# Moving the value products of a group of keys behind the next group's transposes

## The chip, the cores and the metric

The kernel runs on one core of a Trainium2 chip. The metric is the device time of one execution in microseconds (us). Before the change it is 2855.03 us, the median of three runs (2853.68 to 2860.54). The profile comes from one execution of its own.

The engines are PE (TensorE: matrix products and transposes, with PEld for the loading of weights), DVE (VectorE), ACT (ScalarE), POOL (GpSimd) and SP (SyncE, which issues the DMAs here). Each works through its own queue in order. PE writes to PSUM; ACT and DVE read it from there.

## The reference

Two layers (DEPTH) over 2048 frames of width 1024. Each layer normalises x, projects it once, and gives the columns to two groups of four heads; both outputs are concatenated, sent through one output projection, and added to x. A last RMSNorm closes the trunk.

```python
h = rmsnorm(x, norm_w)
proj = einsum('bsd,de->bse', h, w_in)
mq, mk, mv, mi, mf, mz, aq, ak, av, az = split(proj)
# mLSTM heads: causal conv + SiLU on q and k, chunkwise matrix memory, RMSNorm, skip, gate
ym = (rmsnorm(mlstm_chunkwise(conv(mq), conv(mk), mv, mi, mf)) + m_skip * conv(mq)) * silu(mz)
# differential attention: two maps per head, block-causal mask in chunks of 64
p = softmax(where(mask, q k^T / 8, -inf))          # for both maps
a = p[map 0] - lam * p[map 1]
ya = rmsnorm(a @ v) * (1 - lambda_init) * silu(az)
x = x + concat(ym, ya) @ w_out
```

What the change touches is the product `a @ v`, which the text calls the value products. It computes the same numbers before and after.

## The kernel before, in words

**Tiles and units.** The sequence is cut into 4 tiles of 512 frames. A unit is one layer, one tile and one head pair (one mLSTM head and one attention head of the same number): 2 x 4 x 4 = 32 units. All products use operands split in a high and a low part (`hth`/`htl` of the input, `wh`/`wl` of the weights, `ath`/`atl` of the map), three products for one.

**Attention of a unit.** `scores` (L654) computes, for two query blocks of 128 (a pair) and both maps, the scores against all key tiles so far; DVE copies them out of PSUM with their maximum (L706, tile `p`), ACT takes the exponential (L669), and DVE combines the two maps into one (L683). `apply_v` (L722) then handles the combined map in groups of 256 keys. For a group, `ta` (L741) lets PE transpose four blocks of 128 x 128 (L109, tile `tpa`, three blocks at the diagonal, with a memset of the fourth at L748), ACT copies the result out as the high part `ath` (L755), and DVE subtracts it from PSUM to give the low part `atl` (L756). `tb` (L760) then issues the six value products of the group (tile `pv`). There are 288 groups in 64 pairs.

**Buffers.** `tpa` has one buffer in PSUM, `pv` one, `sc` (scores) two, `mm` (projections) three, `ml` one. `ath` and `atl` have two each in SBUF. So the transposes of the next group can begin only when ACT and DVE have both read `tpa`, and a group's copy-out can begin only when the value products two groups before are done.

**The order of the work.** A planner gives every task a due time in its own units, and the tasks are recorded in the order of these times (L1083). Four streams are kept: P (projections and output projections, which fill PE), A (scores), V (transposes, value products, `finish`), and M (the mLSTM). `pin` (L90) ties PE's instructions of a stream into a chain in recorded order; P is also tied behind whatever the other streams had due 15 units earlier. Between the streams a scheduler may order PE's instructions otherwise. On the other engines the copy-outs at L755 and L756 are recorded with a priority of 150 places (`HA`).

The due times of a pair's groups come from `put_v` (L947), with a spacing d of 3 to 6 units:

```python
for i, (ta, tb) in enumerate(gs):
    at(a + i * d, ta, "V")
    at(a + (i + VL) * d, tb, "V")
...
return a + (len(gs) - 1 + VL) * d
```

`VL` is the constant at L40. What `put_v` returns sets the due time of `finish` (L771), of the next pair's first group, and, through `ve + 2.0` and `fin_t`, the earliest due time of the second half of the next value projection and of an output projection.

**The end.** After the last unit, P holds the rest of the output projection of the last tile; its last part (L828 to L845) needs `yha` and `yla` of the last head, which come from the last value products by `ot` (L766), transposes of `ot`, and L792. Then `final_last` (L866) normalises the rows.

Of the kernel before, what the change touches and what calls it, by code (L numbers as in the profile page):

```python
# [36 lines left out]
QL = 0.8  # L37
VF = 0.8
VD = 3.0
VL = 0.6  # L40
FD = 5.5
XD = 10.0
MD = 9.0
# [9 lines left out]
def trunk_kernel(ctx, tc, x, w_ch, w_v0, w_v, w_o, nw, cw, cb, gb, mnw, msk, anw, lam,  # L53
# [893 lines left out]
    def put_v(gs, a, d, groups):  # L947
# [4 lines that stand above are left out]
            if i + 1 == len(gs) or groups[i + 1][0] != groups[i][0]:  # L952
                for _ in range(2):
                    heapq.heappush(p_free, a + i * d + 1.5)
        return a + (len(gs) - 1 + VL) * d

# [212 lines left out]
```

## Time and profile before

| | |
|---|---|
| median of the runs | 2855.03 us |
| the profiled execution | 2855.48 us |
| its span, first to last instruction | 2853.7 us |
| mean granted clock of TensorE | 0.980 of full speed |
| PE busy | 2675.9 us, 94% |
| DVE busy | 1873.5 us, 66% |
| ACT busy | 1641.3 us, 58% |
| POOL busy | 1422.6 us, 50% |

"Idle before" in a row is the time that the engine stood still before that instruction, and the arrow names what ended it. A wait for several things is put down to the last of them. The granted clock is 1.0 at 2.4 GHz and 0.5 at 1.2 GHz.

### The profile page before, as it was taken

The numbers are of one execution on the slowest core, as the hardware profiler recorded it, in microseconds if no ns is written. First come the engines' busy times: TensorE is split into PE (matmuls) and PEld (weight loads), VectorE is DVE, ScalarE is ACT, GpSimd is POOL, SyncE is SP. The second block draws the span as 40 slices with busy tenths as digits, with TensorE's granted clock in tenths as the row PEclk, the third lists the DMA queues.
The fourth block names the chain that finished last, engine by engine and source line by source line (L and its number), as shares of the span: only waits on it lengthen the run. The fifth ranks groups of instructions, "written<-read, shape, count | busy, mean of one in ns | idle before, by whom it ended". The sixth has DMA issues, their size and how long they took to land. (4 is left out here: it accounts for less than half of the span.)

```text
span 2853.7 us, 49241 instructions
## 1 busy us (share of the span) xinstructions
PE 2675.9 (94%) x16692; PEld 2376.0 (83%) x16692; DVE 1873.5 (66%) x4879; ACT 1641.3 (58%) x4407; POOL 1422.6 (50%) x1182
## 2 busy tenths in 40 slices
PE   7999899989999899989999999999999999998997
PEld 6898788878888888977889888888888888887877
DVE  5656565666757757676765466666577676776684
ACT  5555465655655556655655555555465555665664
POOL 5565656535554254434446656555554545445324
PEclk9999999999999999999999999999999999999998
DMA  6645655554653444433546455665447444465232
GB/s 202 173 137 159 187 156 146 152 186 137 181 142 121 152 130 131 140 93 116 163 143 182 141 171 151 198 185 148 144 144 233 139 140 146 115 200 159 82 99 87
DMA packets 248923, 428.91 MB, mean 150 GB/s; under 512 B 30304, under 2 KB 107104, under 8 KB 248672
## 3 DMA queue, kind: packets, MB, share of 16 engines
q1 hardware_dynamic: 248672, 425.77, 50.1%
q8 instruction: 132, 2.16, 0.3%
q14 instruction: 119, 0.97, 0.1%
HBM read 312.28 MB, written 63.05 MB: 132 GB/s over the span
## 5 line engine op out<-in xcount | busy, mean ns | idle before, releaser
L188 POOL TENSOR_TENSOR wl<-wr,wh 128x512 fp32r<-128x512 f32 (+1 forms) x676 | 898.9, 1335 | 1131.2 <-PE mm L106 523.3
L186 ACT ACTIVATE wh<-wr 128x512 fp32r<-128x512 f32 (+1 forms) x676 | 423.0, 628 | 411.0 <-PE mm L106 223.3
L106 PE MATMUL mm<-hth,wh 128*128 128x512 f32 x1536 | 621.7, 405 | 1.6 <-ACT vaug L337 1.4
L106 PE MATMUL mm<-htl,wh 128*128 128x512 f32 x1536 | 610.4, 397 | 0.0
L706 DVE TENSOR_SCALAR_CACHE_REDUCE p<-sc 128x512 f32<-128x512 f32 (+3 forms) x640 | 380.4, 605 | 130.3 <-PE sc L106 115.8
L669 ACT ACTIVATE p<-p,nm 128x512 f32<-128x512 f32 (+3 forms) x640 | 413.7, 649 | 80.8 <-DVE nm L665 79.7
L106 PE MATMUL mm<-hth,wl 128*128 128x512 f32 x1536 | 442.5, 401 | 0.0
L106 PEld LDWEIGHTS mm<-hth,wh 128*128 128x128 f32 x1536 | 292.1, 190 | 60.7 <-ACT vaug L337 2.3
L106 PEld LDWEIGHTS mm<-htl,wh 128*128 128x128 f32 x1536 | 291.7, 190 | 56.9
L106 PEld LDWEIGHTS mm<-hth,wl 128*128 128x128 f32 x1536 | 285.4, 190 | 60.9
L683 DVE SCALAR_TENSOR_TENSOR p<-p,s 128x512 f32<-128x512 f32 (+2 forms) x320 | 293.3, 962 | 2.3
L106 PE MATMUL mm<-wh,hth 128*128 128x256 f32 (+1 forms) x1024 | 268.0, 292 | 19.2 <-DVE gt L339 6.7
L755 ACT ACTIVATE ath<-tpa 128x512 fp32r<-128x512 f32 x288 | 170.4, 592 | 178.2 <-PE tpa L109 176.2
L106 PE MATMUL mm<-wh,htl 128*128 128x256 f32 (+1 forms) x1024 | 263.6, 288 | 0.0
L756 DVE TENSOR_TENSOR atl<-tpa,ath 128x512 fp32r<-128x512 f32 x288 | 197.0, 684 | 88.1 <-ACT ath L755 87.2
L106 PE MATMUL sc<-kp,q 128*128 128x512 f32 x768 | 245.9, 407 | 8.6 <-DVE p L706 8.4
L106 PEld LDWEIGHTS mm<-wh,hth 128*128 128x128 f32 x1024 | 198.8, 194 | 24.7 <-issue 10.7
L106 PEld LDWEIGHTS mm<-wh,htl 128*128 128x128 f32 x1024 | 198.8, 194 | 2.6
L109 PE MATMUL tpa<-ident,p 128*128 128x128 f32 x1088 | 186.6, 278 | 5.9 <-DVE tpa L748 4.5
L400 DVE SCALAR_TENSOR_TENSOR cacc<-mm,cw,cacc 128x511 f32<-128x511 f32 (+2 forms) x192 | 141.5, 737 | 72.2 <-ACT cacc L396 68.9
L106 PE MATMUL pv<-ath,vp 128*128 128x256 f32 x768 | 178.9, 287 | 1.4 <-ACT ath L755 1.4
L106 PE MATMUL mm<-wl,hth 128*128 128x256 f32 (+1 forms) x1024 | 168.6, 293 | 0.6 <-POOL wl L188 0.6
(202 smaller groups left out, 5672.6 us busy)
## 6 DMA issues: line engine op xcount, KB each, us to landing
wr<-in_w_ch_dram SPq DMA_DIRECT2D x384, 256.0 KB, 2.7
wr<-in_w_o_dram SPq DMA_DIRECT2D x132, 256.0 KB, 2.9
q<-ab SPq DMA_DIRECT2D x256, 128.0 KB, 2.4
vp<-vd SPq DMA_DIRECT2D x48, 512.0 KB, 4.5
wr<-in_w_v_dram SPq DMA_DIRECT2D x96, 256.0 KB, 3.4
kp<-kd SPq DMA_DIRECT2D x48, 512.0 KB, 3.7
wr<-in_w_v_dram SPq DMA_DIRECT2D x64, 264.0 KB, 3.1
kc<-ab SPq DMA_DIRECT2D x256, 64.0 KB, 2.0
```

What stands on the lines that cost most here:

```text
L106: pin(PE.matmul(o, l, r, start=start, stop=stop, skip_group_check=True))
L109: pin(PE.transpose(o, i, ident[:n, :n]))
L186: A.activation(wh[:, :n], wr[:, :n], AF.Copy)
L188: G.tensor_tensor(wl[:, :n], wr[:, :n], f32(wh[:, :n]), op=ALU.subtract)
L400: V.scalar_tensor_tensor(out=acc[:, d:], in0=ps[:, 0:T - d], scalar=w(j), in1=acc[:, d:], op0=ALU.mult, op1=ALU.add)
L669: A.activation(pp[:, :w], pp[:, :w], AF.Exp, bias=nm[:, m:m + 1], accum_out=zc[:, m, kt:kt + 1])
L683: V.scalar_tensor_tensor(out=pc[0][kt][:, :w], in0=pc[1][kt][:, :w], scalar=s_[:, 0:1], in1=pc[0][kt][:, :w], op0=ALU.mult, op1=ALU.add)
L706: V.tensor_scalar(out=pp[:, :w], in0=ps[:, :w], scalar1=0.125, scalar2=None, op0=ALU.mult, op1=ALU.max, accum_out=c["mx"][:, m, kt:kt + 1])
L755: A.activation(ah, p2, AF.Copy)
L756: V.tensor_tensor(al, p2, f32(ah), op=ALU.subtract)
```

## The change

One constant is changed; no instruction is added or removed.

```diff
 QL = 0.8
 VF = 0.8
 VD = 3.0
-VL = 0.6
+VL = 1.5
 FD = 5.5
```

A group's value products are due 1.5 spacings after its transposes instead of 0.6, so that the next group's transposes, due one spacing after, come ahead of them in the V chain. `put_v` returns a time that is later by 0.9 d.

PE, inside the attention of layer 1, tile 3, head 2, second pair, before: the transposes of a group (`tpa`), filling products of a projection (`mm`) and of scores (`sc`), then this group's own value products (`pv`), then the next group's transposes.

```order
L109 MATMUL tpa<-ident,p 128x128 x3
L106 MATMUL mm<-hth,wl 128x512 x2
L106 MATMUL mm<-hth,wh 128x512
L106 MATMUL mm<-htl,wh 128x512
L106 MATMUL sc<-kp,q 128x512 x4
L106 MATMUL pv<-ath,vp 128x256
L106 MATMUL pv<-atl,vp 128x256
L106 MATMUL pv<-ath,vp 128x256 x2
L106 MATMUL pv<-atl,vp 128x256
L106 MATMUL pv<-ath,vp 128x256
L109 MATMUL tpa<-ident,p 128x128 x4
```

The same place on PE in the changed kernel, the same names; the value products at the end are those of the first of the two groups.

```order
L109 MATMUL tpa<-ident,p 128x128 x4
L106 MATMUL mm<-hth,wh 128x512
L106 MATMUL mm<-htl,wh 128x512
L106 MATMUL mm<-hth,wh 128x512
L106 MATMUL mm<-htl,wh 128x512
L106 MATMUL mm<-hth,wl 128x512 x4
L106 MATMUL mm<-hth,wh 128x512
L106 MATMUL mm<-htl,wh 128x512
L106 MATMUL mm<-hth,wh 128x512
L106 MATMUL mm<-htl,wh 128x512
L109 MATMUL tpa<-ident,p 128x128 x4
L106 MATMUL pv<-ath,vp 128x256
```

The six value products went from just ahead of the next group's transposes to just behind them, and the first instruction that needs the copied-out group is now the next transposes.

PE at the end of the program, before: the last transposes of a map, four filling products, the last value products, the transposes of `ot`, and the first of the output projection's last part (`wh,yha`).

```order
L109 MATMUL tpa<-ident,p 128x128
L106 MATMUL mm<-wl,yha 128x256 x2
L106 MATMUL mm<-wl,yhm 128x256 x2
L106 MATMUL pv<-ath,vc 128x256
L106 MATMUL pv<-atl,vc 128x256
L106 MATMUL pv<-ath,vc 128x256 x2
L106 MATMUL pv<-atl,vc 128x256
L106 MATMUL pv<-ath,vc 128x256
L109 MATMUL tpa<-ident,ot 128x128 x4
L106 MATMUL mm<-wh,yha 128x256
```

The same end in the changed kernel, from the fillers ahead of the last value products on.

```order
L106 MATMUL mm<-wl,yha 128x256 x2
L106 MATMUL pv<-ath,vc 128x256
L106 MATMUL pv<-atl,vc 128x256
L106 MATMUL pv<-ath,vc 128x256 x2
L106 MATMUL pv<-atl,vc 128x256
L106 MATMUL pv<-ath,vc 128x256
L109 MATMUL tpa<-ident,ot 128x128 x2
L106 MATMUL mm<-wl,yhm 128x256 x2
L106 MATMUL mm<-wh,yhm 128x256
L106 MATMUL mm<-wh,ylm 128x256
L106 MATMUL mm<-wh,yhm 128x256
L106 MATMUL mm<-wh,ylm 128x256
```

Twenty filling products that stood ahead of the last value products now stand behind the first two transposes of `ot`, ahead of the other two.

## Rows read from the trace of the kernel before

**Rows 1.** The page, part 1 and two lines of part 2: busy time (share) and instructions of each engine, then PE's busy tenths and its granted clock in 40 slices of the span.

```profile
PE 2675.9 (94%) x16692; PEld 2376.0 (83%) x16692; DVE 1873.5 (66%) x4879; ACT 1641.3 (58%) x4407; POOL 1422.6 (50%) x1182
...
PE   7999899989999899989999999999999999998997
...
PEclk9999999999999999999999999999999999999998
```

**Rows 2.** The waits of PE over the whole span: who waited for whom, us in total, times, longest us.

```profile
PE pv L106 <- DVE atl L756: 52.8, 35, 5.6
PE mm L109 <- DVE x L239: 15.5, 4, 7.2
PE mm L106 <- DVE htl L273: 14.8, 7, 4.0
PE sc L106 <- DVE p L706: 11.7, 14, 2.5
...
PE pv L106 <- ACT ath L755: 6.4, 10, 2.0
...
PE tpa L109 <- DVE tpa L748: 4.5, 4, 1.6
```

**Rows 3.** PE in order of time in a quiet stretch: start, us, what (neighbours of one kind merged).

```profile
2500.02 0.39 PE L106 MATMUL mm<-htl,wh 128*128 128x512 f32 x1
2500.25 0.39 PE L106 MATMUL mm<-hth,wh 128*128 128x512 f32 x1
...
2501.65 0.28 PE L106 MATMUL pv<-ath,vp 128*128 128x256 f32 x1
2501.77 0.28 PE L106 MATMUL pv<-atl,vp 128*128 128x256 f32 x1
2501.88 0.39 PE L106 MATMUL pv<-ath,vp 128*128 128x256 f32 x2
2502.11 0.29 PE L106 MATMUL pv<-atl,vp 128*128 128x256 f32 x1
2502.24 0.28 PE L106 MATMUL pv<-ath,vp 128*128 128x256 f32 x1
2502.36 0.60 PE L109 MATMUL tpa<-ident,p 128*128 128x128 f32 x4
```

**Rows 4.** PE in order of time around one of the waits, with the idle time before an instruction and what ended it in brackets.

```profile
1294.04 0.28 PE L106 MATMUL pv<-ath,vp 128*128 128x256 f32 x1
1297.35 0.39 PE L106 MATMUL pv<-atl,vp 128*128 128x256 f32 x1 [3.03 <-DVE atl L756]
...
1299.68 0.63 PE L106 MATMUL mm<-hth,wh 128*128 128x512 f32 x1
1300.11 0.63 PE L106 MATMUL mm<-htl,wh 128*128 128x512 f32 x1
```

**Rows 5.** DVE in order of time in three stretches, the first before the wait of rows 4, the second before the longest kind of wait, the third before another wait of 3.0 us.

```profile
1292.70 3.99 DVE L683 SCALAR_TENSOR_TENSOR p<-p,s 128x512 f32<-128x512 f32 x3
1296.61 0.68 DVE L756 TENSOR_TENSOR atl<-tpa,ath 128x512 fp32r<-128x512 f32 x1
...
1214.02 6.75 DVE L683 SCALAR_TENSOR_TENSOR p<-p,s 128x512 f32<-128x512 f32 x4
1220.70 0.68 DVE L756 TENSOR_TENSOR atl<-tpa,ath 128x512 fp32r<-128x512 f32 x1
...
2691.66 4.66 DVE L683 SCALAR_TENSOR_TENSOR p<-p,s 128x512 f32<-128x512 f32 x4
2696.24 0.68 DVE L756 TENSOR_TENSOR atl<-tpa,ath 128x512 fp32r<-128x512 f32 x1
```

**Rows 6.** POOL in order of time beside the second and the third stretch of rows 5.

```profile
1213.92 1.29 POOL L436 TENSOR_TENSOR t<-t,ra 128x512 f32<-128x512 f32 x1
1215.18 1.72 POOL L188 TENSOR_TENSOR wl<-wr,wh 128x512 fp32r<-128x512 f32 x1
1216.85 3.37 POOL L442 TENSOR_TENSOR ab<-t,ab 128x512 fp32r<-128x512 f32 x2
...
2692.82 1.41 POOL L628 TENSOR_TENSOR ylm<-ytm,yhm 128x512 fp32r<-128x512 f32 x1 [1.22 <-ACT yhm L626]
2694.18 1.72 POOL L188 TENSOR_TENSOR wl<-wr,wh 128x512 fp32r<-128x512 f32 x1
```

**Rows 7.** Groups of instructions over the whole span: line, engine, what, count, then busy us, mean ns of one, idle time before and what ended it.

```profile
L683 DVE SCALAR_TENSOR_TENSOR p<-p,s 128x512 f32<-128x512 f32 (+2 forms) x320 | 293.3, 962 | 2.3
L755 ACT ACTIVATE ath<-tpa 128x512 fp32r<-128x512 f32 x288 | 170.4, 592 | 178.2 <-PE tpa L109 176.2
L756 DVE TENSOR_TENSOR atl<-tpa,ath 128x512 fp32r<-128x512 f32 x288 | 197.0, 684 | 88.1 <-ACT ath L755 87.2
```

**Rows 8.** Busy time in ten stretches at half clock, each right behind or around a wait of the value products: stretch and its length, busy us of PE, PEld, DVE, ACT, POOL (instructions), PE's granted clock, DMA share, GB/s; the last line has the sums.

```profile
629.10:639.30 10.20, 6.99 (x32) 6.69 (x32) 6.21 (x11) 3.70 (x9) 6.92 (x6) 0.50 0.51 160
...
1298.10:1301.50 3.40, 3.40 (x12) 2.82 (x11) 1.10 (x3) 0.60 (x1) 0.00 (x0) 0.50 0.07 25
...
2697.56:2700.97 3.41, 3.41 (x13) 2.93 (x12) 1.26 (x3) 0.60 (x1) 0.00 (x0) 0.50 0.09 35
sum 47.65, PE 40.48 PEld 35.16 DVE 28.53 ACT 16.09 POOL 18.66; mean PE 4.05 PEld 3.52 DVE 2.85 ACT 1.61 POOL 1.87
```

**Rows 9.** PE in order of time at the end of the program, from the last value products to the output projection's last part.

```profile
2826.35 0.39 PE L106 MATMUL pv<-ath,vc 128*128 128x256 f32 x1 [0.44 <-ACT ath L755]
2827.29 0.39 PE L106 MATMUL pv<-atl,vc 128*128 128x256 f32 x1 [0.55 <-DVE atl L756]
...
2828.62 0.44 PE L109 MATMUL tpa<-ident,ot 128*128 128x128 f32 x2 [0.25 <-ACT ot L766]
2830.43 0.39 PE L106 MATMUL mm<-wh,yha 128*128 128x256 f32 x1 [1.37 <-ACT yha L626]
2831.77 0.58 PE L106 MATMUL mm<-wh,yla 128*128 128x256 f32 x1 [0.96 <-POOL yla L628]
```

## The prediction

> **What bounds the kernel now.** I read the page first: PE is busy for 94% of the span, DVE, ACT and POOL for no more than 66%, and PE's granted clock falls below nine tenths in none of the 40 slices but the last [rows 1]. So time is won where PE waits, and where its clock is down. Next come PE's own waits. The largest entry is the value products waiting for DVE's subtraction of the low part of the transposed map: 52.8 us in 35 waits, the longest 5.6 us, and 6.4 us more in 10 waits for ACT's copy of the high part [rows 2]. That is 59.2 us; no other entry has more than 15.5 us. The timeline around one wait shows its form: the first value product needs only the high part and runs, the second needs the low part, and PE, which works in order, stands for 3.03 us [rows 4]. Then DVE before such waits: the subtraction itself takes 0.68 us, but it stood behind three or four combinations of the two maps, 3.99, 6.75 and 4.66 us of them [rows 5]. So the wait is a queue on DVE and not the subtraction's own length. Last the clock: behind or around these waits there are ten stretches, 47.65 us together, at half clock; in them PE was busy for 40.48 us [rows 8], and a 512-column product took 0.43 us from start to start [rows 4] where it otherwise takes 0.23 us [rows 3].
>
> **The window.** No instruction is added or removed, so PE's work is the same and only positions count. Before, a group's transposes are followed by filling products, then by this group's six value products, then by the next transposes. Afterwards the same fillers stand there, but the six value products in front of the next transposes are gone, and six of the group before have come in behind the first transposes. The wait does not go: `tpa` has one buffer, so the next transposes wait for the same subtraction in place of the value products. In 225 of the 288 groups they are, by the changed order, the first instruction that needs it; in the others, mostly the last group of a pair or one whose value products moved further, the value products still are. What is won is the length of the window. Six value products take 0.71 us from start to start (2501.65 to 2502.36) [rows 3], and this much work now stands between a group's transposes and the first need of its subtraction that did not stand there before. Counting both orders with the step lengths of rows 3 gives nearly that: the window is 4.3 us on average before and 4.9 us after.
>
> **Its worth in waits.** The 45 waits [rows 2] fall on 37 groups that waited for over 0.2 us and a few that waited less; 25 of the 37 waited longer than 0.71 us. These lose 0.71 us each (17.8 us), the other twelve lose all that they have (5.5 us): 23.3 of the 59.2 us. A second way, place by place: I kept each group's time from transposes to finished subtraction from the trace, and shifted its window by the difference of the two orders at this place. That saves 31.4 us and makes 8.1 us of new waits where the window has become shorter: net 23.3 us too. From one side the change could save nothing, since DVE's queue is refilled differently, and from the other all 59.2 us. I take -23.
>
> **Its worth in clock.** At half clock PE lost half of 40.48 us in those stretches, 20.2 us [rows 8]. 19 waits are over 1.2 us now, and 11 would be after 0.71 us is taken off. In proportion 8 of 19 of 20.2 us is 8.5 us. The long waits, which are the ones that stay, are the surest to be followed by such a stretch, so I take -6, between 0 and 20.
>
> **The end.** After the last value products PE has nothing to fill: it stands for 0.44, 0.55, 0.25, 1.37 and 0.96 us, 3.6 us in all [rows 9]. The changed order puts twenty 256-column products behind the first two transposes of `ot`; at 0.117 us each (the steps of rows 3) this is 2.3 us of work inside that chain. I take -2, between 0 and -3.6.
>
> **What is given back.** On DVE the scheduler's choice changes too. Before, three or more combinations stand among the five rows ahead of a subtraction at 22 places; after, at 33. Of the 22, six waited now, 21.6 us together (the two of 5.5 us and that of rows 4 among them), or 1.0 us for a place. Eleven more places would cost 11 us, and less the share that the longer window takes, 6.5 us; between 0 and 40 (all eleven at the mean 3.6 us of the six). I take +6. Scores have two buffers: the amount by which the PE work between a score tile and its buffer's next use falls short of 2 us adds up to 10.1 us over the order before and 16.6 us after. The wait that answers to it is 11.7 us [rows 2], so +7, between -5 and +15. ACT's side costs nothing: the copy-out takes 0.59 us, and ACT is idle for 178.2 us before it in waiting for the transposes [rows 7]. The buffers of `ath` and `atl` cost nothing either, since the transposes that lead to their reuse stand behind the value products that free them. The later due time of `finish` and of the next value projection shows only in the planner's units, as the projections that wait for it stand many units later; I count 0 for it, up to +5 at the change of layers, where the second half of a value projection is held back by 5 more units.
>
> A rule speaks against the window. The Trainium skill, in "PSUM — Partial Sum Buffer", section "Summary: rules for kernel authors", says that PSUM should be read while matrix products run into a different bank. With one buffer for `tpa` this change does the opposite and puts the next write to that bank in the queue ahead of useful products. By that rule alone the wait would be moved whole and nothing won; no row of before shows transposes waiting for this subtraction, so it stands as the first rival.
>
> A second page prices the queue on DVE higher. Four combinations took 6.75 us while POOL worked without a gap, 1.69 us each [rows 5, 6], against 0.96 us in the mean [rows 7]. The Trainium skill ("SBUF — State Buffer", section "SBUF: two separate sides") has a DVE instruction with two SBUF inputs and a POOL instruction that reads SBUF block each other for whole instructions. The trace agrees at this place. By it a place with four combinations ahead costs 6.8 us instead of 3.8 us, which makes the slower rival dearer by 3 us a place.
>
> **The sum.** -23 -6 -2 +6 +7 = -18 us. Against the profiled execution's own 2855.5 us this is 2837 us. Its time is 0.4 us over the median of the runs, which changes nothing.
>
> **The rivals.** *The wait moves whole* (chance 0.22). The transposes wait instead, DVE's queue being as long relative to PE as before because it is fed by PE's own progress. For it: the copies-out wait for PE for 176.2 us [rows 7], so the engines follow one another; against it: ACT and DVE do not have to wait for value products. Savings of 0 to 9 us, about what the extra places and the scores cost: 2847 to 2864, most likely 2854.
>
> *DVE's queue decides, and the kernel is slower* (0.21). The mechanism is the eleven added places where the subtraction stands behind three or four combinations, now with transposes and everything behind them held. If all cost 3.6 us, this is 40 us, with half clock after each (11 x 1.7 us, half of a 3.4 us stretch) 19 us more, against 31 us saved elsewhere: 2855.5 + 40 + 19 - 31 = 2883; with the half of them 2855.5 + 20 + 10 - 16 = 2869. It decides from about five of the eleven on.
>
> *The longer window clears most waits* (0.12). If the waits go to a quarter, as they might if the scheduler has put the copies-out well at the long waits, 44 us and 13 us of clock go with the 2 us of the end, less 7 us for scores: 2855.5 - 52 = 2803. Against it: the longest waits have four combinations in front and are eight times as long as what is gained.
>
> The forecast has 0.45, with 2815 to 2847 as its own range. A measurement of this kernel tells a difference of about 0.3%, 9 us, from none. Faster by more than that: the forecast's part below 2846.5 and the last rival, 0.56. Within it: 0.23. Slower: the second rival, 0.21. The range leaves out the lower half of the last rival and the upper half of the slower one: 2806 to 2868.
>
> **What would show it.** Right: the value products' wait for the subtraction falls to 15 us or less, a new entry of transposes waiting for the subtraction appears with 15 to 30 us, both together 32 to 42 us; the mean clock rises from 0.980 to about 0.984; scores wait for DVE for 15 to 20 us; PE stands for less than 2 us in the last chain. Wrong: the two waits together are still over 50 us (the wait moved whole) or over 70 us (DVE's queue), or other waits of PE, taken together, grow by more than 15 us.

## The result and the profile after

The changed kernel takes 2882.63 us (median of four runs, 2880.42 to 2891.37) against 2854.53 us before in the same session: on record a ratio of 1.0104, with a 95% interval of 1.0085 to 1.0123 (the two medians alone give 1.0098). It is 1.0% slower. The prediction said 2837 us, 2806 to 2868, and gave "slower" a chance of 0.21; it was wrong in sign, and the time lies outside the range. The ratios here and below leave out two runs that stood far off, one of a control (2979.87 us, at a clock of 0.937) and one of the kernel before (6880.96 us).

The profiled execution took 2883.08 us, its span is 2881.2 us, and the mean granted clock is 0.975 (before: 2855.48, 2853.7, 0.980). The page, part 1 and the two lines of part 2 that answer to [rows 1]:

```profile
PE 2686.6 (93%) x16692; PEld 2380.3 (83%) x16692; DVE 1883.6 (65%) x4879; ACT 1648.2 (57%) x4407; POOL 1426.9 (50%) x1182
...
PE   7999899989998899999999999999999999999987
...
PEclk9999999999999999999999999999999999999999
```

The counts are the same, so the work is. The span grew by 27.5 us: PE's busy time by 10.7 us (the same instructions, at a mean clock of 0.975 instead of 0.980), and its idle time, span less busy, from 177.8 to 194.6 us, 16.8 us more. The waits of PE, to be held against [rows 2] (who waited for whom, us in total, times, longest us):

```profile
PE sc L106 <- DVE p L706: 31.7, 23, 3.3
PE tpa L109 <- DVE atl L756: 30.0, 20, 4.5
...
PE pv L106 <- DVE atl L756: 14.0, 5, 4.3
PE ml L106 <- DVE C L587: 12.8, 7, 2.7
PE tpa L109 <- DVE tpa L748: 12.6, 11, 5.6
...
PE sc L106 <- DMA kc<-ab: 5.7, 2, 5.4
PE sc L106 <- DMA q<-ab: 4.9, 1, 4.9
...
PE pv L106 <- ACT ath L755: 2.3, 2, 1.3
...
PE mm L106 <- DVE htl L273: 1.1, 2, 0.7
```

The entry that the change was aimed at looks as forecast. The value products' 52.8 us became 14.0, the transposes have a new 30.0, and with the wait for `ath` the three fell from 59.2 to 46.3 us, 12.9 us less (a later run shows that this fall is not the swap's). But all other idle time grew by 16.8 + 12.9 = 29.7 us: scores waiting for DVE from 11.7 to 31.7, scores waiting for loads from nothing to 10.6, `ml` for `C` from 4.8 to 12.8, the memset of `tpa` from 4.5 to 12.6; `htl` fell from 14.8 to 1.1. Most of the loss lies in three stretches of layer 1, each between the same two ACT instructions (L423) in both kernels. Their busy times in the kernel before: stretch and length, busy us of PE, PEld, DVE, ACT, POOL (instructions), granted clock, DMA share, GB/s; the last line has the sums:

```profile
2114.90:2227.00 112.10, 108.43 (x698) 97.00 (x698) 86.17 (x217) 71.23 (x207) 53.92 (x44) 0.97 0.67 206
2293.90:2412.70 118.80, 110.57 (x721) 99.64 (x720) 83.64 (x219) 68.41 (x174) 55.49 (x45) 0.97 0.51 154
2483.50:2603.20 119.70, 112.61 (x747) 101.51 (x746) 88.86 (x224) 77.31 (x219) 53.64 (x44) 1.00 0.58 181
sum 350.60, PE 331.61 PEld 298.14 DVE 258.67 ACT 216.96 POOL 163.05; mean PE 110.54 PEld 99.38 DVE 86.22 ACT 72.32 POOL 54.35
```

The same three in the changed kernel:

```profile
2120.20:2242.10 121.90, 109.98 (x698) 98.19 (x697) 88.52 (x218) 70.81 (x205) 53.87 (x44) 0.94 0.60 190
2308.90:2433.70 124.80, 113.80 (x729) 102.45 (x729) 82.09 (x219) 70.15 (x175) 56.47 (x45) 0.95 0.49 147
2502.70:2628.60 125.90, 117.96 (x749) 104.76 (x748) 91.16 (x227) 80.39 (x226) 54.58 (x44) 0.96 0.56 169
sum 372.60, PE 341.74 PEld 305.40 DVE 261.76 ACT 221.35 POOL 164.92; mean PE 113.91 PEld 101.80 DVE 87.25 ACT 73.78 POOL 54.97
```

They are 22.0 of the 27.5 us longer at nearly the same work (2176 products of PE against 2166). Here DVE is busy for 74% of the time before (258.67 of 350.60), against 66% over the whole program. One of the new waits shows how the rest of the order moved. The line is PE's: the first scores of a unit, 5.45 us late, by the profile because the unit's keys (`kc`) are still on the way.

```profile
735.62 2.07 PE L106 MATMUL sc<-kp,q 128*128 128x512 f32 x4 [5.45 <-DMA kc<-ab]
```

Here PE stood ready 0.6 us after the last scores of the unit before; in the kernel before, 11.5 us lay between the two, nearly all of it other work, and there was no wait for the loads. Nothing in the diff speaks of scores. So the theories to tell apart were: the swap of value products and transposes costs (or gains) time by itself; the later due time of a pair's end does; or the order of everything else, which scheduler and planner make afresh after any change, has become worse.

### The profile page after: what moved, and what is told of

It is laid out like the page before. It is cut to its first block, busy times and chain, and to the rows that moved or that the text cites. A ratio compares the mean times of both kernels' runs of the same rounds, so it can differ in the third digit from the quotient of the medians.

```text
span 2881.2 us, 49296 instructions
## 1 busy us (share of the span) xinstructions
PE 2686.6 (93%) x16692; PEld 2380.3 (83%) x16692; DVE 1883.6 (65%) x4879; ACT 1648.2 (57%) x4407; POOL 1426.9 (50%) x1182
## 4 chain that ended last, share of the span: by engine, by line
PE 58%; DVE 12%; DMA 7%; ACT 3%; issue 2%; POOL 1%; SPq 0%; POOLq 0%; ACTq 0%; DVEq 0%
PE mm L106 39%; PE sc L106 6%; PE pv L106 5%; PE tpa L109 4%; DVE p L683 4%; PE ml L106 2%; DMA bc<-bw 2%; DMA x<-xo 1%; DVE p L706 1%; ACT p L669 1%; DVE cacc L400 1%; DVE atl L756 1%; DMA x<-in_x_dram 1%; DVE x L265 1%; DVE cacc L402 1%
## 5 line engine op out<-in xcount | busy, mean ns | idle before, releaser
L188 POOL TENSOR_TENSOR wl<-wr,wh 128x512 fp32r<-128x512 f32 (+1 forms) x676 | 902.7, 1341 | 1125.1 <-PE mm L106 485.5
L106 PE MATMUL mm<-hth,wh 128*128 128x512 f32 x1536 | 614.8, 400 | 4.2 <-ACT vaug L337 4.2
L106 PE MATMUL mm<-hth,wl 128*128 128x512 f32 x1536 | 436.3, 398 | 0.0
L106 PEld LDWEIGHTS mm<-wh,hth 128*128 128x128 f32 x1024 | 199.0, 194 | 20.3 <-issue 7.5
L109 PEld LDWEIGHTS tpa<-ident,p 128*128 128x128 f32 x1088 | 135.4, 143 | 84.2 <-DVE atl L756 22.5
L106 PE MATMUL pv<-ath,vp 128*128 128x256 f32 x768 | 190.8, 310 | 0.0
```

The costliest lines, as they stand in the source:

```text
L106: pin(PE.matmul(o, l, r, start=start, stop=stop, skip_group_check=True))
L109: pin(PE.transpose(o, i, ident[:n, :n]))
L188: G.tensor_tensor(wl[:, :n], wr[:, :n], f32(wh[:, :n]), op=ALU.subtract)
```

## The experiments

### Other values of the constant

Four kernels move the value products by other amounts.

**0.55:** a little earlier than before.

```diff
-VL = 0.6
+VL = 0.55
```

> VL = 0.55: the value products stay ahead of the next transposes and are due a twentieth of a spacing earlier, so neither the swap nor the lateness is in it, only a newly made order. Swap theory (the wait moves whole to the transposes and costs more there): 2850 to 2860, as before. Lateness theory (the pair's chain ends 0.9 of a spacing later): 2850 to 2860. Fresh-order theory (the order of before happens to be a good one, and any other due time gives one with more waits elsewhere, the scores above all): 2870 to 2890, scores waiting for DVE 20 us or more where it was 11.7.

**0.95:** as late as can be while they still stand ahead of the next transposes, so no swap.

```diff
-VL = 0.6
+VL = 0.95
```

> VL = 0.95: the value products stand just ahead of the next transposes, so no swap, but due 0.35 of a spacing later. Swap theory: about 2855. Lateness theory: a third of the loss, about 2865. Fresh-order theory: 2870 to 2890.

**1.05:** just behind the next transposes, so the swap and little more.

```diff
-VL = 0.6
+VL = 1.05
```

> VL = 1.05: the value products stand just behind the next transposes, due 0.1 of a spacing later than with 0.95 and 0.45 earlier than in the changed kernel. Swap theory: about 2880, clearly slower than with 0.95, and the transposes' wait for the subtraction near 30 us. Lateness theory: half of the loss, 2868. Fresh-order theory: 2865 to 2890, not told apart from 0.95.

**Swap without a later pair's end:** 1.5, but the last group of a pair and what `put_v` returns stay at 0.6.

```diff
-VL = 0.6
+VL = 1.5
...
-            at(a + (i + VL) * d, tb, "V")
+            at(a + (i + (VL if i + 1 < len(gs) else 0.6)) * d, tb, "V")
...
-        return a + (len(gs) - 1 + VL) * d
+        return a + (len(gs) - 1 + 0.6) * d
```

> VL = 1.5, but the last group of each pair keeps 0.6, and the pair's chain ends where it did before: the swap without the lateness. Swap theory: about 2880. Lateness theory: 2845 to 2858. Fresh-order theory: 2865 to 2890.

Measured: 1.0049 of before (1.0031 to 1.0067), 1.0119 (1.0092 to 1.0146), 1.0099 (1.0078 to 1.0120) and 1.0107 (1.0090 to 1.0124). At 0.95 nothing is swapped and it is as slow as 1.05 and 1.5; with the pair's end back at 0.6 it is as slow as without. So the loss needs neither the swap nor the later end, and 0.05 less costs 13 us though nothing that these theories name has changed. Each of these four has an order of its own, though, so they don't tell what the swap or the later end is worth by itself. What they point to is the order made afresh.

### The order held fixed

To move one thing and nothing else, the order in which each engine takes its instructions was read from a kernel, written out as a table, and chained on every engine; the planner's own chain falls away. Such an edge fixes the order of issue and adds no wait.

```diff
-        tc.add_manual_dep(r.ins, name, nosync, reason="TensorE order")
+        pass
...
         f()
+    _pinned(tc, nc)
...
+def _pinned(tc, nc):
...
+            if prev is not None:
+                tc.add_manual_dep(i, prev.name, nosync, reason="written order")
+            prev = i
```

**Controls:** the order of before, and the order of the changed kernel, with nothing moved.

> A control. The order that the kernel before has on each of its five engines is written out, row by row, in the kernel and replaces the planner's edges; nothing is moved. Every theory expects the time of before, 2850 to 2860 us. If it is off by more than 5 us, the edges with which an order is written out cost something themselves, and the two kernels that follow are to be read against this one.

> A control: the changed kernel's own order written out on all five engines, nothing moved. Expected by every theory: as the changed kernel, 1.0085 to 1.0123 of before, 2878 to 2893. If it is off by more, the three runs with one thing moved on this order are to be read against this one.

Measured: 0.9995 (0.9979 to 1.0010) and 1.0108 (1.0095 to 1.0121), as the kernels whose orders they are. The table itself costs nothing that these runs can tell.

**The swap alone**, on the order of before, as at 224 groups on PE:

```diff
+L109 MATMUL tpa<-ident,p 128x128 x2
 L106 MATMUL pv<-ath,vc 128x256
 L106 MATMUL pv<-atl,vc 128x256
...
-L109 MATMUL tpa<-ident,p 128x128 x2
```

> The order of before written out on all five engines, with one thing moved: on TensorE, at 224 groups, the six value products stand right behind the next group's transposes. No other row of any engine moves. The forecast's own step (the six products' 0.71 us lie inside the window that the wait for the subtraction has, and clear 25 of 37 waits): 23 us less than before, 2825 to 2840. Wait moves whole: the transposes wait as long as the products did, 2850 to 2860, with the wait of the value products (43.6 us of before) now at the transposes. Swap costs by itself: over 2865, with the waits for the subtraction above 60 us. The order made afresh is to blame: not over 2860 here, since nothing else moved.

Measured: 1.0001 (0.9986 to 1.0015). No gain, no loss. The waits of PE for the subtraction in this run:

```profile
PE tpa L109 <- DVE atl L756: 35.9, 24, 4.1
PE pv L106 <- DVE atl L756: 16.4, 11, 5.5
```

35.9 + 16.4 = 52.3 us, against the 52.8 of [rows 2]: the wait moved whole. Why is seen at the place of [rows 4], here in this run. PE, in order of time:

```profile
1290.57 0.60 PE L109 MATMUL tpa<-ident,p 128*128 128x128 f32 x4
1290.92 0.36 PE L106 MATMUL pv<-ath,vp 128*128 128x256 f32 x1
...
1293.80 0.40 PE L106 MATMUL mm<-htl,wh 128*128 128x512 f32 x1
1297.32 0.94 PE L109 MATMUL tpa<-ident,p 128*128 128x128 f32 x4 [3.13 <-DVE atl L756]
```

ACT's copy and DVE at the same place of this run:

```profile
1291.54 0.58 ACT L755 ACTIVATE ath<-tpa 128x512 fp32r<-128x512 f32 x1
...
1292.01 4.66 DVE L683 SCALAR_TENSOR_TENSOR p<-p,s 128x512 f32<-128x512 f32 x4
1296.59 0.68 DVE L756 TENSOR_TENSOR atl<-tpa,ath 128x512 fp32r<-128x512 f32 x1
```

And in the kernel before:

```profile
1291.28 0.60 PE L109 MATMUL tpa<-ident,p 128*128 128x128 f32 x4
...
1291.97 0.60 ACT L755 ACTIVATE ath<-tpa 128x512 fp32r<-128x512 f32 x1 [0.18 <-PE tpa L109]
...
1292.03 4.66 DVE L683 SCALAR_TENSOR_TENSOR p<-p,s 128x512 f32<-128x512 f32 x4
```

The swap did what it says: the transposes begin 0.71 us earlier and the copy ends 0.45 us earlier. But the four combinations begin at the same time in both (the row in [rows 5] has three of them because its window begins later), the subtraction stands behind them, and it begins at 1296.59 instead of 1296.61. PE has done the same work by the time it needs the result, in another order, and waits as long: 3.13 us in place of 3.03.

That is one of three forms. In the second, the copy itself comes no earlier, because ACT goes to it straight from other work. PE and ACT around one of the waits, before:

```profile
1088.78 0.60 PE L109 MATMUL tpa<-ident,p 128*128 128x128 f32 x4
1091.36 0.19 ACT L590 ACTIVATION_READ_ACCUMULATOR mjunk<-hs 128x1 f32 x1
1091.45 0.58 ACT L755 ACTIVATE ath<-tpa 128x512 fp32r<-128x512 f32 x1
```

And with the swap:

```profile
1085.71 0.60 PE L109 MATMUL tpa<-ident,p 128*128 128x128 f32 x4
1089.01 0.19 ACT L590 ACTIVATION_READ_ACCUMULATOR mjunk<-hs 128x1 f32 x1
1089.10 0.58 ACT L755 ACTIVATE ath<-tpa 128x512 fp32r<-128x512 f32 x1
```

The copy begins 2.67 us after the first transpose before and 3.39 us after it now; the wait was 1.24 us and is 1.36. In the third form a group has three transposes. Only the first two went ahead; the last, which the copy needs as well, stands behind the same fillers as before. Such a group is that of the wait of 5.5 us in the second stretch of [rows 5]; before:

```profile
1212.07 0.38 PE L109 MATMUL tpa<-ident,p 128*128 128x128 f32 x2
1213.67 0.27 PE L109 MATMUL tpa<-ident,p 128*128 128x128 f32 x1
1214.04 0.60 ACT L755 ACTIVATE ath<-tpa 128x512 fp32r<-128x512 f32 x1
```

And with the swap:

```profile
1209.93 0.38 PE L109 MATMUL tpa<-ident,p 128*128 128x128 f32 x2
1212.26 0.27 PE L109 MATMUL tpa<-ident,p 128*128 128x128 f32 x1
1212.62 0.60 ACT L755 ACTIVATE ath<-tpa 128x512 fp32r<-128x512 f32 x1
```

Counted over both traces: of the 35 groups that PE waited for before, 26 have their transposes ahead of the value products now. In 21 of these the time from the first transpose to the finished subtraction grew by 0.4 to 1.1 us, 0.71 us in the mean, which is all that the transposes had won: nine times with the last transpose behind the same fillers, eight times with the copy straight behind other work of ACT, four times mainly in DVE's queue. The waits for these 21 were 36.5 us and are 36.9. DVE's queue adds to most waits in both kernels: in that of before the subtraction began more than 0.15 us after its copy's end in 31 of the 35, which hold 51.5 of the 52.8 us, and each time DVE went straight from another instruction to it.

**The changed kernel's order without the swap:** its value products put back ahead of the next transposes at 224 groups.

```diff
+L106 MATMUL pv<-ath,vc 128x256 x2
+L106 MATMUL pv<-atl,vc 128x256
+L106 MATMUL pv<-ath,vc 128x256
 L109 MATMUL tpa<-ident,p 128x128 x2
...
-L106 MATMUL pv<-ath,vc 128x256 x2
-L106 MATMUL pv<-atl,vc 128x256
-L106 MATMUL pv<-ath,vc 128x256
```

> The order of the changed kernel written out on all five engines, with the six value products of 224 groups moved back to stand just ahead of the next group's transposes; nothing else moves. The order made afresh is to blame: as slow as the changed kernel or slower, 2878 to 2900, and the other waits of TensorE (scores for the exponents' maxima above 28 us, ml for C above 10 us) stay as in the changed kernel. Swap costs by itself: the time of before, 2850 to 2862. The forecast's window is right by its sign: 10 to 23 us slower than the changed kernel, 2892 to 2906.

Measured: 1.0159 (1.0139 to 1.0180). This is the order of the changed kernel without the change that was meant, and it is the slowest so far: 45 us over before (0.0159 x 2854.5). So the order made afresh is to blame. But the time lies in the range of the third expectation too: against its control of 1.0108 the swap gives back 0.5% there, 12 us between the medians (2899.51 and 2887.45). It does not do so by the waits that it was aimed at. Those for the subtraction are 43.9 us here without the swap and 47.1 us in the control with it, so the fall from 52.8 to 44.0 us in the changed kernel is the new order's. In the profiled executions PE's busy time for the same instructions is 11.6 us shorter with the swap (2698.5 and 2686.9 us, mean clock 0.973 and 0.976), its idle time 5.4 us.

### Taking single waits away

**Subtractions ahead of the combinations**, the second rival's mechanism: on DVE, at 32 places of the changed kernel's order.

```diff
+L756 TENSOR_TENSOR atl<-tpa,ath 128x512
 L683 SCALAR_TENSOR_TENSOR p<-p,s_8801 128x512 x3
-L756 TENSOR_TENSOR atl<-tpa,ath 128x512
```

> The order of the changed kernel written out on all five engines, with one thing moved on VectorE: at 32 places at which three or more combinations (L683) stand in the five rows ahead of a subtraction (L756), the subtraction goes ahead of them, 139 rows passed in all. VectorE's queue decides (my second rival): the waits for the subtraction at places with three combinations ahead, 29.2 us in the changed kernel, fall below 10, and the time by 15 to 25 us, to 2858 to 2868. The order made afresh in many places is to blame: these waits fall as well, but a maps' combination that comes 2 us later is waited for elsewhere, and the time falls by less than 10 us, 2873 to 2885.

Measured: 1.0123 (1.0100 to 1.0146), no faster than the control; the median of 2891.11 us lies above both expected ranges. At places with three or more combinations ahead the waits were 29.2 us in the changed kernel; now none is left, and all waits for the subtraction went from 44.0 to 23.1. But the scores took it up:

```profile
PE sc L106 <- DVE p L706: 49.0, 31, 5.3
PE tpa L109 <- DVE atl L756: 22.8, 19, 4.3
```

**Scores later**, at 22 places where they waited in the changed kernel; on PE:

```diff
-L106 MATMUL sc<-kc,q 128x256 x2
 L106 MATMUL mm<-wh,hth 128x256
 L106 MATMUL mm<-wh,htl 128x256
...
+L106 MATMUL sc<-kc,q 128x256 x2
```

> The order of the changed kernel written out on all five engines, with one thing moved on TensorE: the 22 pairs of score products that waited over 0.4 us for VectorE's eviction (L706) or for a load, 41 us in all, stand later by as much other TensorE work as they had waited (with those that follow them closely, 38 pairs in all). No other engine's order moves. Crowded scores are what the remade order costs: their waits fall from 31.7 us (L706) and 10.6 us (loads) to under 12 and under 3 us, and the time falls by 20 to 40 us, to 2842 to 2862. Waits only change their place: these waits fall, others (subtraction, the memset of tpa, C) grow by as much, and the time stays within 10 us of the changed kernel, 2873 to 2890.

Measured: 1.0174 (1.0152 to 1.0195), slower than the control by 0.65% and above both expected ranges. The scores' wait did go, to 4.3 us and none for loads. The subtraction's rose from 44 to 59.7 us, and new ones came up behind the later softmax (`nm`) and the weights' copies (`wh`):

```profile
PE tpa L109 <- DVE atl L756: 38.3, 22, 4.5
PE pv L106 <- DVE atl L756: 21.4, 8, 4.3
...
PE tpa L109 <- DVE nm L665: 12.4, 4, 4.1
PE mm L106 <- ACT wh L186: 10.2, 7, 2.3
...
PE sc L106 <- DVE p L706: 4.3, 9, 1.3
```

**The same on the order of before:** 21 subtractions ahead of the combinations, without the swap and with it.

```diff
+L756 TENSOR_TENSOR atl<-tpa,ath 128x512
 L683 SCALAR_TENSOR_TENSOR p<-p,s_9793 128x512 x2
 L683 SCALAR_TENSOR_TENSOR p<-p,s_9793 128x384
-L756 TENSOR_TENSOR atl<-tpa,ath 128x512
```

> The order of before written out on all five engines, with 21 subtractions (L756) moved on VectorE ahead of the three or four combinations (L683) that stood in front of them, 88 rows passed. VectorE's queue decides: the 21.7 us of waits at these places fall below 5, and the time by 10 to 20 us, to 2833 to 2843. Waits change their place (as in the changed kernel, where the same edit took 21 us of waits away and put 17 us on the scores): 2850 to 2868.

> Both edits at once on the order of before: the value products behind the next transposes at 224 groups, and the 21 subtractions ahead of the combinations. If VectorE's full queue at these places is all that made the swap worth nothing: 5 to 15 us less than with the subtractions moved alone. If the subtraction is late because VectorE is busy with other rows at nearly all of the waits, so that earlier transposes don't make it earlier: within 5 us of the run with the subtractions moved alone.

Measured: 0.9996 (0.9983 to 1.0009) and 0.9937 (0.9913 to 0.9962). Alone, the edit halves the subtraction's waits and hands them to the scores:

```profile
PE sc L106 <- DVE p L706: 29.1, 21, 3.8
PE pv L106 <- DVE atl L756: 27.6, 30, 3.9
```

With the swap on top the kernel is 0.6% faster than before and than the run without it, 2839.5 us, with 0.65 (below) the fastest measured; yet its waits for the subtraction are no shorter (23.8 + 6.5 us):

```profile
PE sc L106 <- DVE p L706: 25.4, 17, 3.4
PE tpa L109 <- DVE atl L756: 23.8, 23, 4.0
...
PE pv L106 <- DVE atl L756: 6.5, 10, 1.2
```

So the gain has the size that was expected of a freed queue, 15 us between the medians, but not its path. Here too most of it is busy time: PE's is 12.2 us shorter in the profiled execution (2681.6 and 2669.4 us, mean clock 0.979 and 0.981), its idle time 7.2 us. How the place of the value products does this was not found. Whether it holds elsewhere was tried on the order of 0.65, next.

### Chance or lateness

**0.65**, a small step to the other side, and **0.8**, between it and 0.95.

```diff
-VL = 0.6
+VL = 0.65
```

> The constant at 0.65 instead of 0.6, nothing written out: value products still stand ahead of the next transposes, and the planner makes the order afresh. The order made afresh is a draw, and that of before a good one: over 2862, as 0.55 (2869.6) on the other side. The later the value products, the slower (a smooth rise from 0.6 to 1.5, 28 us over 0.9): within 5 us of before, 2850 to 2858.

```diff
-VL = 0.6
+VL = 0.8
```

> The constant at 0.8, between 0.65 (0.995 of before) and 0.95 (1.012): value products still ahead of the next transposes, order made afresh. Lateness with a slope: half way, 1.000 to 1.007, 2855 to 2875. Chance: anywhere between 0.993 and 1.013, and no information from its neighbours.

Measured: 0.9950 (0.9931 to 0.9969) and 1.0089 (1.0064 to 1.0113). 0.65 is faster than before, with 49.1 us of waits for the subtraction, near the 52.8 of before. Both expectations were missed: the first theory's bound (over 2862 us) was wrong in side, and right only in that 0.05 moves the time by 0.5%. 0.8 missed the range of the slope (1.000 to 1.007).

**Another constant**: the memory chain is due 9.2 or 8.8 instead of 9.0 after the convolved projections of its unit (by the code; the expectations say after its gates). It is `M`'s, and no due time of the value products depends on it.

```diff
-MD = 9.0
+MD = 9.2
```

> The kernel before (0.6) with another constant changed: the memory chain's work is due 9.2 instead of 9.0 after its gates. Nothing of the value products' placing changes, but the planner makes the order afresh (TensorE's lists differ in 5654 lines, against 6078 for 0.65 and 21618 for the changed kernel). Chance: off before by more than 8 us, either way. Lateness of the value products is what costs: within 6 us of before, 2848 to 2861.

```diff
-MD = 9.0
+MD = 8.8
```

> The same constant at 8.8, so a third order with the value products placed as before (6347 lines of TensorE's list differ). Chance: off before by more than 8 us, and not by the same as at 9.2. Lateness: within 6 us of before, 2848 to 2861.

Measured: 1.0116 (1.0093 to 1.0139) and 1.0065 (1.0040 to 1.0090). A constant that leaves the value products alone costs 1.2% and 0.7%, against the 1.0% of the change under study. The waits that grew are others again: in the first the scores (18.7 us, against 11.7) and `htl` (20.3, against 14.8), in the second the subtraction itself:

```profile
PE pv L106 <- DVE atl L756: 66.3, 42, 5.8
```

**The same on the changed kernel:** 1.5, and the memory chain at 9.2.

```diff
-MD = 9.0
+MD = 9.2
```

> The changed kernel (1.5) with the memory chain's work due 9.2 instead of 9.0 after its gates: another order with the same late value products (TensorE's list differs from the changed kernel's in 8665 lines). Chance: off the changed kernel by more than 8 us, either way, so below 2874 or above 2891. Later value products as such are what costs: within 8 us of the changed kernel.

Measured: 1.0046 (1.0025 to 1.0067). The same swap, as late as in the changed kernel, and 0.6% faster than it, as the first expectation has it.

**Both edits on the order of 0.65:** the swap at 224 groups and 26 subtractions ahead of the combinations.

```diff
+L756 TENSOR_TENSOR atl<-tpa,ath 128x512
 L683 SCALAR_TENSOR_TENSOR p<-p,s_9793 128x512 x2
 L683 SCALAR_TENSOR_TENSOR p<-p,s_9793 128x384
-L756 TENSOR_TENSOR atl<-tpa,ath 128x512
```

> The order of the kernel with 0.65 written out on all five engines, and on it both edits: the value products behind the next transposes at 224 groups, and the subtractions ahead of three or more combinations at 26 places (109 rows passed). If the two edits together are worth 0.6% on any order, as on that of before: 2820 to 2830 (0.989 of before). If their gain on the order of before was chance as well: 2836 to 2860.

Measured: 0.9949 (0.9927 to 0.9972), the time of 0.65 without them. The 0.6% on the order of before is not a gain that the two edits bring on any order.

## Why the prediction was wrong

**The cause.** Ten kernels had their order made afresh, seven by other values of the constant (one of them with the pair's end kept), two by another chain's constant, one by both. In the traces "swapped" is at 224 groups or at none. They took, of before:

| what was changed | swapped | ratio |
|---|---|---|
| 0.65 | no | 0.9950 |
| 1.5, memory chain 9.2 | yes | 1.0046 |
| 0.55 | no | 1.0049 |
| memory chain 8.8 | no | 1.0065 |
| 0.8 | no | 1.0089 |
| 1.05 | yes | 1.0099 |
| 1.5 (the change) | yes | 1.0104 |
| 1.5, pair's end at 0.6 | yes | 1.0107 |
| memory chain 9.2 | no | 1.0116 |
| 0.95 | no | 1.0119 |

Nine of the ten are slower than before, by 0.7% in the mean of all ten; the four with the swap have a mean of 1.0089, the six without 1.0065, and either group spreads over more than that difference. With every other order held, the swap was worth 0.0% on the order of before, -0.5% on that of the changed kernel, and -0.6% on that of before with the subtractions ahead; in none of the three did it cost time. So the 28 us are no price of the swap. They come with giving up the order of before for one made afresh, and unrelated constants cost as much. Whether a later due time by itself has a part in them is not settled: the six kernels due at 0.8 or later have a mean of 1.0094, the four at 0.65 or earlier 1.0045, a difference of half the loss, but the four alone spread from 0.9950 to 1.0116. What makes the order of before a good one was not found: two waits that had grown were taken away, each by itself, and each time other waits took their place and the kernel was no faster.

**The window, -23.** This is the step that failed first: "These lose 0.71 us each (17.8 us)". The order did put about that much work into the window, but the subtraction's end was taken to follow the group's first transposes by a fixed time. It did not follow them: the last transpose, ACT's queue or DVE's queue kept it where it was, 0.71 us later after the first transpose than before. The prediction itself says at its start that "the wait is a queue on DVE", from [rows 5], where combinations run for 4 to 7 us right up to the subtraction; the sum then left that out. "ACT's side costs nothing" is wrong too: it was read from ACT's idle time over all groups, and at eight of the waits ACT came to the copy straight from other work. The second way, place by place, was no check: it kept the time from transposes to finished subtraction, the same assumption. With the order held the wait went from 52.8 to 52.3 us, and on the two other orders it rose with the swap, from 43.9 to 47.1 and from 27.6 to 30.3 us.

**The clock, -6.** It went the other way, from 0.980 to 0.975, and PE's busy time for the same instructions grew by 10.7 us. PE's idle time grew as well; that the one comes from the other is not shown.

**The end, -2.** Of the five waits of [rows 9] two are left, 0.68 us for `yha` and 2.39 us for `yla`, 3.1 us instead of 3.6: -0.5. POOL began `yla` at once before, and in the changed kernel only behind a splitting of weights (L188, 2.50 us).

**DVE's queue, +6.** By the five DVE instructions ahead there are 21 such places in the trace before and 28 after, 7 more where the prediction counted 11 more, and their waits grew by 8.0 us, 21.2 to 29.2. So the size was right, but as a price it meant nothing: without these waits the time was the same (1.0123 against 1.0108).

**Scores, +7.** The sign was right, the size was not: 20.0 us more, and 10.6 us for loads that were not foreseen. Again no price: with 38 of these 42 us gone the kernel was slower.

**What was counted at next to nothing.** This is the second step that failed, and the one that made the sign wrong. The planner's and scheduler's new order of everything else stood in the sum as two counts, 6 and 7 us, and the later due times as 0. It was worth 45 us, by the run that has it without the swap; no term or rival had it.

**The rivals.** *The wait moves whole* described the swap on the order of before exactly (52.3 us, 1.0001); its text has only DVE's queue for the reason, which is one of three. The Trainium skill ("PSUM — Partial Sum Buffer", "Summary: rules for kernel authors") asks that PSUM be read while matrix products run into another bank. The trace agrees in that the transposes into the one `tpa` buffer now wait 35.9 us for its reading. A second buffer for `tpa` was not tried: it would not make the subtraction earlier, but by the program these transposes would not have to wait for it, and what that is worth is open. *DVE's queue decides* gave 2883 us, the time that was measured, for a cause that the runs don't bear out: with the waits at these places gone the time was the same. *The longer window clears most waits* asked for a quarter of 59.2 us to be left; 46.3 are. Of the signs listed as wrong the last one came: other waits grew by 29.7 us, where 15 was the mark, while the two waits aimed at came out at 44.0 us, near the 32 to 42 of the forecast. Those two entries looked right by luck, since the same order without the swap has 43.9 us, and they told nothing of the time.

## What to carry to other kernels

Before a wait is shortened by giving its producer an earlier start, look at every step up to the producer: whether its last input comes earlier and not only the first, and whether each engine on the way was idle when its input came. Where one went from an instruction straight to the next, an earlier input only waits longer. Where a planner and a scheduler make the order afresh after any edit, change first a constant that has nothing to do with the idea, to see how far the time moves by itself (here +0.7% and +1.2%), and test the idea on an order that is written out and held. A wait that disappears from the list is no gain until the time says so: here each that was taken away by itself came back under another name.

## What the runs showed that was not expected

The scatter itself: 0.05 in one due time, or 0.2 in another, moved the time of a program with the same work by up to 35 us (2856 to 2891 us). And in two edits the waits behave as if their sum belonged to the order: moving 21 or 32 subtractions took 25 and 21 us from their own entry and put 17 us on the scores, both times, and the time stayed within 0.2%. The swap, with two orders held, shortened PE's busy time by 12 us for the same instructions without shortening the waits that it was made for; why is open.
